# First token block gathered row by row; two dense blocks with some plain fp32 products

## The chip, the cores and the metric

One core of one Trainium2 chip. The metric is the device time of one execution in microseconds. Engines: TensorE (PE) for matrix products, VectorE (DVE) and ScalarE (ACT) for elementwise work, GpSimd (POOL), which here only issues the gathers, and SyncE (SP), which issues the other DMA transfers.

## The reference, cut to what matters

```python
h  = rms_norm(x, norm1_gain)                       # 512 tokens x 1024
A  = dsa_attention(...)                            # sparse attention, indexer picks keys
B  = gated_deltanet(...)                           # chunked, sequential over 64 tokens
x += W_o @ (sigmoid(gA) * (A @ W_A) + sigmoid(gB) * (B @ W_B))
h2 = rms_norm(x, norm2_gain)
# PEER: 8 heads, product keys, top 16 of 128*128 experts per head and token
q  = (h2 @ w_query).reshape(ntok, 8, 2, 128)
s  = einsum('nhpd,hpkd->nhpk', q, sub_keys)        # 128 scores per half
top_s, top_i = top_k(s, 16)                        # per half, then 16 of 16x16 sums
x += sum over the 128 chosen experts e of gate[e] * gelu(h2 . u[e]) * v[e]
```

All of it is fp32. The tables u and v have 16384 rows of 1024 numbers each (64 MB apiece).

## The kernel before, in words

The 512 tokens are four blocks of 128. The program is written with helpers that record each operation; the framework's scheduler then fixes an order for each engine. In place of one plain fp32 product, `mm3` (L91) makes three f32r products from operands that `split` (L167 on ACT, L168 on DVE) cuts into a high and a low part: high x high, high x low, low x high.

- **Projections and chains (first stage).** `fill` is a stream of filler steps: 43 slices of w_in by `mm3`, convolutions, then `attention_branch` (the attention half of the merge, f32r on all 512 tokens). It is interleaved with the four chains (`deltanet` for two pairs of heads, `indexer`, `attender`), FILL_A filler steps for each chain step until the attention's inputs are there, FILL_B after that. `szT` and `qT` hold the chains' results.
- **Merge.** For each of 8 slices the DeltaNet half is multiplied (L709), added (L710), split; then w_o, `second_norm` (L714) for each block, and `hT` (transposed, high and low).
- **Routing.** w_q's products, scores, top 16 of 128 by DVE (L857 to L861), and `choose` (16 best sums, their gates and expert numbers) for each block.
- **Two ways of applying experts.** Blocks 0, 1, 2 are WHOLE: `spread` makes dense gates with one-hot outer products (oa, ob, L983, L986, product `wo`) and writes them to DRAM (gd); `dense_u(i)` multiplies 128 experts' u by the three blocks (24 f32r products of 384 columns) and takes gelu; `dense_v(i)` multiplies the gated activations by 128 rows of v (18 f32r products of 512 columns into six accumulators `acc`). Block 3 is GATHERED: `gathered(s)` fetches, for choice s of each of 128 tokens, one row of 8 KB (u and v side by side) by an indirect DMA of POOL (L951), then a dot (L960) and an addition (L963) on DVE.
- **Order.** AHEAD + KEPT = 62 of the 128 `dense_u` run early (during routing and spread); KEPT = 42 of these write their activations to DRAM (gs) to be read back. The other 66 run in the last stage, spread between the 128 `dense_v`, and so do the gathered rows; U_COST and V_COST space them. Row buffers: ROWS = 4.

Names in the rows: wt, wh, wl a weight tile and its parts; ut, uh, ul those of u; vt, vh, vl those of v; gt, ch, cl the gates; hTh, hTl the input; ya, yh, yl the merge's inputs; row a gathered row; a__ the result of a `dense_u`.

## Time and profile before

| what | value |
|---|---|
| median of 3 runs | 1850.85 us (1849.44 to 1852.79) |
| profiled execution | 1844.26 us, its span 1842.5 us |
| granted clock, mean | 0.998 |
| PE busy | 1791.8 us (97%) |
| DVE busy | 1442.0 us (78%) |
| ACT busy | 803.1 us (44%) |
| DMA moved | 396.74 MB, 215 GB/s on average |

Times are microseconds from the start of the span. "Busy" is the union of an engine's instructions. An instruction's length in the groups contains its latency, so lengths of neighbours overlap. A chain piece "x36" is a run of 36 instructions of one engine. The DMA share is that of 16 DMA engines; it can read slightly over 1.

### The profile page before, as it was taken

The numbers are of one execution on the slowest core, as the hardware profiler recorded it, in microseconds if no ns is written. First come the engines' busy times: TensorE is split into PE (matmuls) and PEld (weight loads), VectorE is DVE, ScalarE is ACT, GpSimd is POOL, SyncE is SP. The second block draws the span as 40 slices with busy tenths as digits, with TensorE's granted clock in tenths as the row PEclk, the third lists the DMA queues.
The fourth block names the chain that finished last, engine by engine and source line by source line (L and its number), as shares of the span: only waits on it lengthen the run. The fifth ranks groups of instructions, "written<-read, shape, count | busy, mean of one in ns | idle before, by whom it ended". The sixth has DMA issues, their size and how long they took to land.

```text
span 1842.5 us, 26292 instructions
## 1 busy us (share of the span) xinstructions
PE 1791.8 (97%) x9527; PEld 1572.5 (85%) x9527; DVE 1442.0 (78%) x3291; ACT 803.1 (44%) x1401; POOL 188.6 (10%) x132
## 2 busy tenths in 40 slices
PE   5999999999999999999999999999999999999998
PEld 4787677878788899999999988888888888888887
DVE  5767988654667899999997686788787887787886
ACT  5433434443533334555655444344443444343442
POOL 0000000000000000010000112122121222212220
PEclk9999999999999999999999999999999999999999
DMA  4211111111643214567676898989988988898974
GB/s 148 92 64 63 58 41 58 52 52 41 211 147 130 89 52 142 186 226 258 250 268 228 307 365 305 336 316 361 337 313 327 347 315 309 335 357 313 343 299 170
DMA packets 142354, 396.74 MB, mean 215 GB/s; under 512 B 10704, under 2 KB 71760, under 8 KB 122768
## 3 DMA queue, kind: packets, MB, share of 16 engines
q1 hardware_dynamic: 123792, 260.84, 40.3%
q0 software_dynamic: 18432, 134.23, 18.9%
q8 instruction: 75, 1.23, 0.3%
q14 instruction: 55, 0.45, 0.1%
HBM read 353.60 MB, written 41.29 MB: 214 GB/s over the span
## 4 chain that ended last, share of the span: by engine, by line
PE 82%; DVE 8%; DMA 6%; ACT 2%; issue 1%; SPq 0%; DVEq 0%; ACTq 0%
PE mm L91 28%; PE acc L91 25%; PE wo L91 6%; PE dn L91 5%; PE at L91 3%; DMA vt<-in_uv_dram 2%; DMA gt<-gd 2%; DVE ul L168 1%; DVE ob L986 1%; PE tr L91 1%; PE at L571 0%; PE dn L320 0%; DMA wt<-in_w_br_dram 0%; DVE tmp L229 0%; DVE gt L1046 0%
## 5 line engine op out<-in xcount | busy, mean ns | idle before, releaser
L91 PE MATMUL acc<-vl,ch 128*128 128x512 f32 x768 | 299.5, 390 | 1.1 <-DVE vl L1045 1.1
L91 PE MATMUL acc<-vh,cl 128*128 128x512 f32 x768 | 298.2, 389 | 0.0
L91 PE MATMUL acc<-vh,ch 128*128 128x512 f32 x768 | 263.1, 390 | 4.9 <-ACT vh L1044 4.9
L951 POOL DMA_INDIRECT row<-in_uv_dram,eidx x124 | 178.6, 1441 | 832.3 <-DVE x1g L963 775.1
L167 ACT CAST uh<-ut 128x1024 fp32r<-128x1024 f32 x128 | 134.6, 1051 | 150.0 <-PE mm L91 84.0
L1045 DVE TENSOR_TENSOR vl<-vt,vh 128x1024 fp32r<-128x1024 f32 x128 | 156.4, 1222 | 50.3 <-ACT vh L1044 47.6
L168 DVE TENSOR_TENSOR ul<-ut,uh 128x1024 fp32r<-128x1024 f32 x128 | 155.9, 1219 | 34.4 <-ACT uh L167 33.8
L91 PE MATMUL mm<-hTh,uh 128*128 128x384 f32 x496 | 168.6, 340 | 2.9 <-ACT gs L818 1.9
L91 PEld LDWEIGHTS acc<-vh,ch 128*128 128x128 f32 x768 | 143.3, 188 | 32.1 <-ACT vh L1044 6.6
L91 PE MATMUL mm<-hTh,ul 128*128 128x384 f32 x496 | 168.0, 340 | 2.7 <-DVE ul L168 2.7
L91 PEld LDWEIGHTS acc<-vl,ch 128*128 128x128 f32 x768 | 144.2, 188 | 30.2 <-DVE vl L1045 2.1
L963 DVE SCALAR_TENSOR_TENSOR x1g<-row,co,x1g 128x1024 f32<-128x1024 f32 x128 | 163.8, 1280 | 7.4 <-ACT co L962 5.3
L91 PEld LDWEIGHTS acc<-vh,cl 128*128 128x128 f32 x768 | 144.1, 188 | 29.2
L1044 ACT CAST vh<-vt 128x1024 fp32r<-128x1024 f32 x128 | 133.9, 1046 | 78.4 <-DMA vt<-in_uv_dram 64.0
L91 PE MATMUL mm<-hTl,uh 128*128 128x384 f32 x496 | 167.3, 337 | 0.0
L167 ACT CAST ch<-gt 128x384 fp32r<-128x384 f32 x128 | 65.5, 512 | 218.1 <-PE acc L91 211.1
L960 DVE CUSTOM_DVE_ANT_0 scr<-row,h2g 128x1024 f32<-128x1024 f32 x128 | 156.0, 1218 | 0.3
L91 PE MATMUL mm<-hh,wh 128*128 128x512 f32 x344 | 144.6, 424 | 3.6 <-ACT hh L167 2.1
L168 DVE TENSOR_TENSOR wl<-wt,wh 128x1024 fp32r<-128x1024 f32 (+1 forms) x81 | 90.1, 1115 | 63.4 <-ACT wh L167 63.2
L91 PE MATMUL mm<-hh,wl 128*128 128x512 f32 x344 | 137.3, 401 | 0.0
L91 PE MATMUL mm<-hl,wh 128*128 128x512 f32 x344 | 136.9, 398 | 0.0
L167 ACT CAST wh<-wt 128x1024 fp32r<-128x1024 f32 (+1 forms) x81 | 77.7, 962 | 110.9 <-PE mm L91 86.7
(818 smaller groups left out, 3765.8 us busy)
## 6 DMA issues: line engine op xcount, KB each, us to landing
ut<-in_uT_dram SPq DMA_DIRECT2D x128, 512.0 KB
vt<-in_uv_dram SPq DMA_DIRECT2D x128, 512.0 KB
gd<-gb SPq DMA_DIRECT2D x24, 1024.0 KB
gt<-gd SPq DMA_DIRECT2D x16, 1536.0 KB
wt<-in_w_in_dram SPq DMA_DIRECT2D x43, 512.0 KB
gs<-gs SPq DMA_DIRECT2D x84, 192.0 KB
wt<-in_w_q_dram SPq DMA_DIRECT2D x16, 512.0 KB
sgd<-tmp SPq DMA_DIRECT2D x16, 256.0 KB
```

Of the source, the lines that this page charges most:

```text
L91: hop[0] = PE.matmul(o, l, r, start=start, stop=stop).ins
L167: S.copy(hi, src)
L168: return V.tensor_tensor(lo, src, hi.bitcast(F32), op=ALU.subtract).ins
L951: G.indirect_dma_start(out=row.rearrange("p t d -> p (t d)"), out_offset=None, in_=uv, in_offset=bass.IndirectOffsetOnAxis(ap=released.get ...
L960: V.tensor_tensor_reduce(scr, row[:, 0], h2g, 1.0, 0.0, op0=ALU.mult, op1=ALU.add, accum_out=a)
L963: V.scalar_tensor_tensor(x1g, row[:, 1], co, x1g, op0=ALU.mult, op1=ALU.add)
L986: V.tensor_scalar(ob[:, t], io, sl[:, 1, n:n + 1], sl[:, 2, n:n + 1], op0=ALU.is_equal, op1=ALU.mult)
L1044: S.copy(vh, vt)
L1045: paced = V.tensor_tensor(vl, vt, vh.bitcast(F32), op=ALU.subtract)
```

## The change

Block 0 leaves the dense blocks: FIRST = 0, WHOLE = (1, 2), GATHERED = 3. `first_block` merges, norms and routes block 0 alone, in the filler stream behind the projections, as soon as the chains have done its tokens, all of it by plain fp32 products (`mm`, one product instead of three); it reads w_br, w_o and w_q a second time (4.2 + 4.2 + 8.4 MB). `first_rows` then gathers block 0's experts: 128 half rows of u (4 KB for each of 128 tokens, 0.5 MB a gather) with a dot on DVE, gelu and gate, 128 half rows of v with an addition. `rows(n)` takes n steps of that stream: it is called in the filler, the merge, the routing, the spread, with each gathered row of block 3, and for what is left at the end. The half rows share four buffers (tag "row").

The dense parts are 256 columns wide now. `dense_u` is 8 plain fp32 products (no split of u); `dense_v` is 12 f32r products, and for every third row (PLAIN = 3, 42 of 128) 4 plain ones without any split. AHEAD 34, KEPT 14. The merge has one loop with both halves on 384 columns, and `attention_branch` is gone.

```diff
-WHOLE, GATHERED = (0, 1, 2), 3
+FIRST, WHOLE, GATHERED = 0, (1, 2), 3
+REST = (*WHOLE, GATHERED)
 NU = len(WHOLE) * P
-FILL_A = 0.85
-FILL_B = 0.6
+NR = len(REST) * P
+FILL_A = 1.0
+FILL_B = 1.3
...
-AHEAD = 20
-KEPT = 42
+AHEAD = 34
+KEPT = 14
...
-V_COST, U_COST = 18 * T, 24 * NU
+V_COST, U_COST = 12 * 227, 16 * 222
+PLAIN = 3
+STEPS = 4
...
+    def first_block():
+        while not done >= {("y", 0, i) for i in range(3)}:
+            yield
+        c = slice(0, P)
+        quarter = lambda n: hp.tile([P, 8, P], F32, name=n, tag="hh", bufs=4)
+        m0 = quarter("m0")
         for dt in range(8):
             s_ = tmp()
-            load(s_, sgd[dt])
-            S.activation(s_, s_, AF.Sigmoid)
-            wt = pp.tile([P, 8, P], F32, name="wt", bufs=2)[:, :4]
-            load(wt, w_br[dt][:, :4])
-            w = [pp.tile([P, 8, P], F32R, name=n, bufs=2)[:, :4] for n in ("wh", "wl")]
-            split(*w, wt)
+            for i in range(2):
+                load(hs(s_, i), sgd[8 * i + dt][:, c])
+            S.activation(s_[:, :2 * P], s_[:, :2 * P], AF.Sigmoid)
+            w = plain(w_br[dt])
...
+                yield
+            V.tensor_tensor(s_[:, :2 * P], s_[:, :2 * P], o[:, :2 * P], op=ALU.mult)
+            V.tensor_tensor(m0[:, dt, :], hs(s_, 0), hs(s_, 1), op=ALU.add)
...
+        for cg in range(2):
+            o = bank("mm")
+            for kp_ in range(4):
+                w = plain(w_o[cg, kp_], (2, T))
+                for k in range(2):
+                    kk = 2 * kp_ + k
+                    mm(o, m0[:, kk, :], w[:, k, :], kk == 0, kk == 7)
+                    yield
+            half = slice(cg * T, (cg + 1) * T)
+            V.tensor_tensor(x1[:, half], x1[:, half], o, op=ALU.add)
...
+        srs = lists[:, 2]
+        for h in range(8):
+            o = bank("mm")
+            for p in range(2):
+                w = plain(w_q[2 * h + p])
+                for k in range(8):
+                    mm(hs(o, p), w[:, k, :], h0[:, k, :], k == 0, k == 7)
+                    if k % 4 == 3:
+                        yield
+            q_ = tmp()
+            load(q_[:, 2 * P:].rearrange("p (l k) -> p l k", k=P), subT[:, 2 * h:2 * h + 2, :])
+            S.copy(q_[:, :2 * P], o[:, :2 * P])
...
+            for p in range(2):
+                t_, i_ = ts[FIRST][:, p, h], ti[FIRST][:, p, h]
+                best(hs(sc, p), t_[:, 0:8], t_[:, 8:16], i_[:, 0:8], i_[:, 8:16], srs[:, p])
...
+        choose(FIRST, new)
...
+        V.scalar_tensor_tensor(first["eu"], flat(sel[FIRST][0]), 256.0, ef, op0=ALU.mult, op1=ALU.add)
...
+    def row_of(s, which):
+        r = ep.tile([P, D], F32, name="row_f", tag="row", bufs=ROWS)
+        G.indirect_dma_start(
+            out=r,
+            out_offset=None,
+            in_=uv2,
+            in_offset=bass.IndirectOffsetOnAxis(ap=first[which][:, s:s + 1], axis=0),
+        )
+        return r
+    def first_rows():
+        a = first["a"]
+        for s in range(P):
+            r = row_of(s, "eu")
+            V.tensor_tensor_reduce(r, r, first["h2"], 1.0, 0.0, op0=ALU.mult, op1=ALU.add, accum_out=a[:, s:s + 1])
+            yield
...
+        for s in range(P):
+            r = row_of(s, "ev")
+            V.scalar_tensor_tensor(first["x1"], r, a[:, s:s + 1], first["x1"], op0=ALU.mult, op1=ALU.add)
+            yield
+        nc.sync.dma_start(out[0:P, :], first["x1"])
...
+    def rows(n):
+        for _ in range(n):
+            next(rows_f, None)
...
         yield from projections()
-        while "mixed" not in done:
-            yield
-        yield from attention_branch()
+        yield from first_block()
+        for _ in range(P):
+            rows(1)
+            for _ in range(STEPS):
+                yield
...
+    while "x1" not in first:
+        next(filler)
...
+        s_ = [tmp() for _ in range(2)]
+        o = [bank("mm")[:, :NR], bank("tr")[:, :NR]]
+        w = weights(pp, w_br[dt])
+        for i in range(2):
+            load(s_[i][:, :NR], sgd[8 * i + dt][:, rest])
+            S.activation(s_[i][:, :NR], s_[i][:, :NR], AF.Sigmoid)
+            for k in range(4):
+                y = (ya[k][:, 0], ya[k][:, 1]) if i == 0 else at(yd, k)
+                mm3(o[i], at(w, 4 * i + k), y, k == 0, k == 3)
+            V.tensor_tensor(s_[i][:, :NR], s_[i][:, :NR], o[i], op=ALU.mult)
+        m_ = s_[0][:, :NR]
+        V.tensor_tensor(m_, m_, s_[1][:, :NR], op=ALU.add)
+        split(mt[0][:, dt, :], mt[1][:, dt, :], m_)
+        rows(2)
...
+        rows(2)
...
+                rows(1)
...
-        ut = up.tile([P, 8, P], F32, name="ut", bufs=2)
+        ut = up.tile([P, 8, P], F32, name="ut", bufs=3)
         load(ut, uT[i])
-        uh = up.tile([P, 8, P], F32R, name="uh", bufs=2)
-        ul = up.tile([P, 8, P], F32R, name="ul", bufs=2)
-        split(uh, ul, ut)
         for k in range(8):
-            mm3(a_, (uh[:, k, :], ul[:, k, :]), (hT[0][:, k, :NU], hT[1][:, k, :NU]), k == 0, k == 7)
+            mm(a_, ut[:, k, :], hT1[:, k, :], k == 0, k == 7)
...
+            rows(1)
...
-        scr = rowq.tile([P, D], F32, name="scr", bufs=1)
-        V.tensor_tensor_reduce(scr, row[:, 0], h2g, 1.0, 0.0, op0=ALU.mult, op1=ALU.add, accum_out=a)
+        V.tensor_tensor_reduce(row[:, 0], row[:, 0], h2g, 1.0, 0.0, op0=ALU.mult, op1=ALU.add, accum_out=a)
...
+            rows(3)
...
     def dense_v(i):
         if i % IC == 0:
-            gt[0] = ex.tile([P, NCH, IC, TC], F32, name="gt", bufs=2)
+            gt[0] = lp.tile([P, NCH, IC, TC], F32, name="gt", tag="big", bufs=2)
             load(gt[0].rearrange("p c i n -> p c (i n)"), gd.rearrange("c p k -> p c k")[:, :, i * TC:(i + IC) * TC])
         g = gt[0][:, :, i % IC, :]
-        vt = ex.tile([P, D], F32, name="vt", bufs=2)
+        vt = ex.tile([P, D], F32, name="vt", bufs=3)
         load(vt, uv[i * P:(i + 1) * P, D:])
+        ge = activations(i)
+        if i % PLAIN == PLAIN - 1:
+            paced = V.tensor_tensor(ge.rearrange("p (c n) -> p c n", n=TC), ge.rearrange("p (c n) -> p c n", n=TC), g, op=ALU.mult)
+            for j, b in enumerate(WHOLE):
+                for c in range(2):
+                    mm(acc[b][c], hs(ge, j), vt[:, c * T:(c + 1) * T], i == 0, i == P - 1)
+            return paced
+        paced = V.tensor_tensor(g, ge.rearrange("p (c n) -> p c n", n=TC), g, op=ALU.mult)
         vh = ex.tile([P, D], F32R, name="vh", bufs=2)
         vl = ex.tile([P, D], F32R, name="vl", bufs=2)
-        S.copy(vh, vt)
-        paced = V.tensor_tensor(vl, vt, vh.bitcast(F32), op=ALU.subtract)
-        V.tensor_tensor(g, activations(i).rearrange("p (c n) -> p c n", n=TC), g, op=ALU.mult)
+        split(vh, vl, vt)
         ch = ex.tile([P, NCH, TC], F32R, name="ch", bufs=2)
         cl = ex.tile([P, NCH, TC], F32R, name="cl", bufs=2)
         split(ch, cl, g)
         chf, clf = (a.rearrange("p c n -> p (c n)") for a in (ch, cl))
-        for b in WHOLE:
+        for j, b in enumerate(WHOLE):
             for c in range(2):
-                mm3(acc[b][c], (hs(chf, b), hs(clf, b)), (vh[:, c * T:(c + 1) * T], vl[:, c * T:(c + 1) * T]), i == 0, i == P - 1)
+                half = slice(c * T, (c + 1) * T)
+                mm3(acc[b][c], (hs(chf, j), hs(clf, j)), (vh[:, half], vl[:, half]), i == 0, i == P - 1)
         return paced
...
+                rows(1)
+    for _ in rows_f:
+        pass
```

How the rows move, engine by engine (before, then now).

**DVE, the end of the last DeltaNet chain.** L329/L330 and L342/L343 start the norm of the last output, rs_t, rs_a, r are the steps of its inverse root, `ot` the output; L849 is the new dot with a gathered half row. Before:

```order
L329 TENSOR_REDUCE s_4139<-s_4137 128x2
L330 TENSOR_SCALAR s_4139<-s_4139 128x2
L159 TENSOR_SCALAR rs_t<-s_4139 128x2
L634 TENSOR_TENSOR mixed<-tmp,mm 128x512
L160 TENSOR_SCALAR r_4142<-rs_t 128x2
L168 TENSOR_TENSOR wl<-wt,wh 128x512
L162 TENSOR_TENSOR rs_a<-r_4142 128x2
L163 SCALAR_TENSOR_TENSOR rs_t<-rs_a,s_4139 128x2
```

Now:

```order
L463 SCALAR_TENSOR_TENSOR szT<-dn_4736,colv,szT 128x2x128
L849 ISA row_f,a_f<-row_f,xe 128x1024
L849 ISA a_f 128x1
L342 TENSOR_REDUCE s_4839<-s_4837 128x2
L849 ISA row_f,a_f<-row_f,xe 128x1024
L849 ISA a_f 128x1
L343 TENSOR_SCALAR s_4839<-s_4839 128x2
L849 ISA row_f,a_f<-row_f,xe 128x1024
L849 ISA a_f 128x1
L171 TENSOR_SCALAR rs_t<-s_4839 128x2
L172 TENSOR_SCALAR r_4842<-rs_t 128x2
```

The dots, each with a read of its sum (L849 ISA a_f), stand between the norm's steps; the first stands one row ahead of these. Of the 128 dots 118 stand ahead of the spread: 10 up to the last step of this chain, the others between the merge's and the routing's rows.

**POOL, the gathers.** Before, 4 and 124 gathers of 8 KB rows and nothing else. Now:

```order
L836 DMA row_f<-in_uv_dram,eu 128x1024 x122
L1117 DMA row<-in_uv_dram,free 128x2048 x4
L1117 DMA row<-in_uv_dram,eidx 128x2048 x6
L836 DMA row_f<-in_uv_dram,eu 128x1024 x4
L1117 DMA row<-in_uv_dram,eidx 128x2048
L836 DMA row_f<-in_uv_dram,eu 128x1024 x2
L1117 DMA row<-in_uv_dram,eidx 128x2048
L836 DMA row_f<-in_uv_dram,ev 128x1024 x2
```

`row_f` is a half row of block 0 (eu from u, ev from v), `row` a whole row of block 3. All 128 half rows of v stand behind the first gathers of block 3; from there on the two kinds alternate until the end.

**PE, the last stage.** `acc` are the accumulators of `dense_v`, `a__` the result of a `dense_u`. Before, a row of u is 24 rows, a row of v 18, of which six stand together:

```order
L91 MATMUL a__11837<-hTh,uh 128x384
L91 MATMUL a__11837<-hTl,uh 128x384
L91 MATMUL a__11837<-hTh,ul 128x384
L91 MATMUL acc_9964<-vh,ch 128x512
L91 MATMUL acc_9965<-vh,ch 128x512
L91 MATMUL acc_9966<-vh,ch 128x512
L91 MATMUL acc_9967<-vh,ch 128x512
```

Now, with two rows of u, a plain row of v and the start of a split one:

```order
L98 MATMUL a__10246<-hT_4878,ut 128x256 x8
L98 MATMUL a__10327<-hT_4878,ut 128x256 x8
L98 MATMUL acc_8694<-vt,ge 128x512
L98 MATMUL acc_8695<-vt,ge 128x512
L98 MATMUL acc_8696<-vt,ge 128x512
L98 MATMUL acc_8697<-vt,ge 128x512
L98 MATMUL acc_8694<-vh,ch 128x512
L98 MATMUL acc_8695<-vh,ch 128x512
```

A row of u takes its operand `ut` straight from the load; a plain row of v takes `vt` and `ge` so.

## Rows read from the trace of the kernel before

**Rows 1.** Windows by stage: us; PE, PEld, DVE, ACT, POOL busy; clock; DMA share; GB/s.
```profile
0.00:487.00 487.00, 460.10 (x2477) 363.89 (x2478) 330.20 (x901) 210.59 (x408) 0.20 (x4) 1.00 0.22 74
487.00:580.00 93.00, 88.87 (x431) 74.96 (x429) 61.01 (x121) 35.86 (x54) 0.00 (x0) 0.98 0.45 158
580.00:755.00 175.00, 171.63 (x923) 157.60 (x922) 159.23 (x832) 67.80 (x108) 0.00 (x0) 0.99 0.31 104
755.00:1030.00 275.00, 270.88 (x1827) 269.58 (x1826) 246.53 (x619) 159.70 (x203) 17.65 (x10) 1.00 0.67 242
1030.00:1842.50 812.50, 800.36 (x3877) 706.42 (x3876) 645.07 (x821) 329.15 (x630) 170.77 (x118) 1.00 0.88 322
```

**Rows 2.** The chain that ended last, by engine.
```profile
PE 82%; DVE 8%; DMA 6%; ACT 2%; issue 1%; SPq 0%; DVEq 0%; ACTq 0%
```

**Rows 3.** The chain in the last stage: start us, us, what.
```profile
1074.99 17.22 DMA vt<-in_uv_dram
```

**Rows 4.** Windows with full DMA engines, and a long one (columns as above).
```profile
1084.00:1094.00 10.00, 9.37 (x48) 8.23 (x47) 5.84 (x12) 1.77 (x3) 0.94 (x1) 1.00 1.01 413
1240.00:1260.00 20.00, 20.00 (x101) 17.99 (x100) 18.57 (x26) 8.89 (x17) 4.52 (x4) 1.00 1.01 401
1030.00:1090.00 60.00, 59.05 (x290) 52.37 (x290) 50.06 (x68) 25.23 (x47) 14.10 (x9) 1.00 1.02 377
1420.00:1620.00 200.00, 199.44 (x974) 177.05 (x973) 159.29 (x202) 81.01 (x156) 48.08 (x32) 1.00 0.89 328
```

**Rows 5.** DMA issues in 1030 to 1090 us: KB each.
```profile
gt<-gd SPq DMA_DIRECT2D x2, 1536.0 KB
```

**Rows 6.** The chain, two pieces of the last stage.
```profile
1441.42 8.16 PE acc L91 x36
1449.58 4.19 PE a__13633 L91 x24
```

**Rows 7.** PE by line and form, first stage: xcount, busy us, mean ns.
```profile
L91 PE MATMUL at<-kT,qT 64*128 64x512 f32 x16 | 9.0, 641 | 0.0
L91 PE MATMUL at<-kT,qT 64*128 64x256 f32 x16 | 5.6, 428 | 0.0
```

**Rows 8.** PE by line and form, 0 to 487 us.
```profile
L91 PE MATMUL mm<-ya,wh 128*128 128x512 f32 x53 | 17.6, 405 | 0.6 <-ACT ya L167 0.3 <-ACT wh L167 0.2
L91 PE MATMUL mm<-ya,wl 128*128 128x512 f32 x26 | 10.2, 398 | 0.0
```

**Rows 9.** DVE by line and form, 580 to 755 us.
```profile
L168 DVE TENSOR_TENSOR ul<-ut,uh 128x1024 fp32r<-128x1024 f32 x18 | 21.8, 1214 | 0.0
L858 DVE FIND_INDEX8 ti<-ts,sc 128x8 uint32<-128x128 f32 x64 | 17.9, 286 | 0.0
L861 DVE MATCH_VALUE_LOAD ti<-ts,sr 128x8 f32 x64 | 4.8, 75 | 0.0
```

**Rows 10.** DVE's timeline at the end of the chains: start us, us, instruction.
```profile
478.02 0.17 DVE L330 TENSOR_SCALAR s<-s 128x2 f32<-128x2 f32 x1
486.16 0.48 DVE L450 SCALAR_TENSOR_TENSOR szT<-dn,colv,szT 128x256 f32<-128x256 f32 x1
```

**Rows 11.** DMA of the last stage, and the landing time of gathered rows.
```profile
DMA packets 98874, 259.93 MB, mean 325 GB/s; under 512 B 5984, under 2 KB 58629, under 8 KB 83717
row<-in_uv_dram,eidx POOLq DMA_INDIRECT x118, 8.7
```

**Rows 12.** DVE by line and form, last stage.
```profile
L1045 DVE TENSOR_TENSOR vl<-vt,vh 128x1024 fp32r<-128x1024 f32 x128 | 156.4, 1222 | 50.3 <-ACT vh L1044 47.6 <-issue 2.3
L963 DVE SCALAR_TENSOR_TENSOR x1g<-row,co,x1g 128x1024 f32<-128x1024 f32 x122 | 156.1, 1280 | 5.2 <-ACT co L962 3.2
L960 DVE CUSTOM_DVE_ANT_0 scr<-row,h2g 128x1024 f32<-128x1024 f32 x122 | 148.6, 1218 | 0.3
L168 DVE TENSOR_TENSOR cl<-gt,ch 128x384 fp32r<-128x384 f32 x128 | 70.9, 554 | 42.9 <-ACT ch L167 42.5
L960 DVE DVE_READ_ACCUMULATOR2_ANT a<- 128x1 f32 x122 | 10.0, 82 | 0.0
```

**Rows 13.** POOL's gathers.
```profile
L951 POOL DMA_INDIRECT row<-in_uv_dram,eidx x124 | 178.6, 1441 | 832.3 <-DVE x1g L963 775.1 <-DVE ob L986 51.6 <-issue 2.7
```

More of the change, by code (lines that the diff above doesn't have):

```diff
@@ new lines, in tile_block, with plain @@
+    x1d = [dr.tile([P, D], F32, name=f"x1d{b}") for b in WHOLE]
+    first = {}
+    uv2 = uv.rearrange("e (t d) -> (e t) d", t=2)
+    turn_w = [0]
+    def plain(src, shape=(8, P)):
+        turn_w[0] += 1
+        n = ("wt", "wh", "wl")[turn_w[0] % 3]
+        w = pp.tile([P, *shape], F32, name=f"p{n}", tag=n, bufs=2)
+        load(w, src)
+        return w
+    def first_block():
[4 more added lines that the diff above has]
+        m0 = quarter("m0")
@@ L630, in attention_branch @@
+        r2 = tiny.tile([P, 1], F32, name="r2e")
+        S.activation(h2, x1, AF.Square, accum_out=s1)
+        V.tensor_scalar(s1, s1, 1.0 / D, EPS, op0=ALU.mult, op1=ALU.add)
+        rsqrt(r2, s1, "e")
+        V.scalar_tensor_tensor(h2, x1, r2, n2g, op0=ALU.mult, op1=ALU.mult)
+        h0 = quarter("h0")
+        for half in range(2):
+            p_ = bank("mm")
             for k in range(4):
-                mm3(o, at(w, k), (ya[:, 0, k], ya[:, 1, k]), k == 0, k == 3)
-                if k < 3:
-                    yield
@@ new lines, in first_block @@
+        sel[FIRST] = [new(f"sel{i}", [P, 8, 16]) for i in range(2)]
+        gate[FIRST] = ep.tile([P, 8, 16], F32, name="gate_f")
+        choose(FIRST, new)
+        ef = new("ef", [P, P])
+        for i, n in enumerate(("eu", "ev")):
+            first[n] = ep.tile([P, P], I32, name=n)
+        V.tensor_scalar(ef, flat(sel[FIRST][1]), 2.0, None, op0=ALU.mult)
+        V.scalar_tensor_tensor(first["eu"], flat(sel[FIRST][0]), 256.0, ef, op0=ALU.mult, op1=ALU.add)
+        V.tensor_scalar(ef, ef, 1.0, None, op0=ALU.add)
@@ L672, in tile_block @@
                     next(filler, None)
-    for _ in filler:
-        pass
+    while "x1" not in first:
+        next(filler)
     show("yaT", qT)
@@ L768, in tile_block @@
                 w[kp_] = weights(pp, w_o[cg, kp_], shape=(2, T))
-            for b in range(NB):
-                with behind(turned[b - NLAG] if b >= NLAG else None):
+            for b in REST:
+                with behind(turned.get(b - NLAG)):
                     for kp_ in range(4):
```

354 lines of the change are left out of this document (202 added, 152 removed).

## The prediction, made before the changed kernel ran

> **What bounds the kernel now.** I read the stages first, from the table of windows [rows 1]. TensorE (PE) is busy 460 of 487 us in the first stage, 89 of 93 in the merge, 172 of 175 in the routing, 271 of 275 while the gates are spread and 800 of 812 in the last stage; the chain of waits says the same, 82% of it on PE [rows 2]. So before, TensorE is the end of every stage. But two other columns of the same table matter for this change: VectorE (DVE) is busy 645 of the last 812 us, and the DMA engines have a share of 0.88 there at 322 GB/s. The chain shows that this share is no longer free cover: at 1075 us PE waits 17.2 us for a row of v [rows 3].
>
> **How fast the DMA engines can go** is read where their share is 1.0 or more [rows 4]: 413 GB/s over 10 us, 401 over 20 us, 377 over 60 us. In the 60 us two of the gate transfers were issued (gt, 1.5 MB, by the code in pieces of 512 bytes) [rows 5]; in the two faster windows none. Over 200 us in which PE was busy 199.4, the rate was 328 GB/s at a share of 0.89.
>
> **Prices on PE.** An f32r product of 512 columns takes 8.16/36 = 0.227 us, one of 384 columns 4.19/24 = 0.174 us [rows 6]. A plain fp32 product shows as two instructions. Their lengths are 641 and 428 ns for 512 and 256 columns [rows 7]; the difference gives 0.213 us of engine time for 256 columns, so 0.427 for 512 and 0.107 for 128. Lengths overlap, so differences and back-to-back pieces are the price, not the lengths.
>
> **The change, part by part.**
>
> *First stage.* Block 0 gets its own merge, w_o, w_q and scores in plain fp32: 64 products of 128 columns for w_br (128 x 0.107 = 14 us), 16 of 512 for w_o (32 x 0.427 = 14), 128 for w_q (256 x 0.107 = 27), 16 for the scores (3): 58 us of PE. Taken away are the attention half's products, which move into the merge: 53 + 26 of 512 columns [rows 8], 79 x 0.227 = 18. Net +40; PE was idle 27 us in this stage, and I let none of it be filled: 527. The bounds are 507 (20 of the 27 idle us get filled) and 555. Block 0's top-16 is a quarter of the 98 us of eight groups, of which the first and the last stand in [rows 9] (17.9 and 4.8), 25 us of DVE, and with its choose about 45, beside 330 of 487 busy: hidden.
>
> The order shows something that the words of the change don't: the first dot with a gathered row stands at the very end of the chains, and 10 dots stand one to one between the tiny steps of the last chain's norm. In the trace those steps lie between 478.0 and 486.2 us [rows 10]. DVE is in order, so each now waits for a gather. One gather's cost from both sides: 8.7 us to land [rows 11] plus a dot of 1.3 over four buffers is 2.5 us; below it is the dot alone, 1.3. I take 2.0 (these rows are 0.5 MB where those were 1 MB): 10 x 2 = 20 us, half of it covered by the merge's first products. +10, with 0 and 25 as ends. The first stage ends at 537.
>
> *Merge and routing* (268 us before). DVE was busy 61 + 159 = 220 [rows 1]. Less 22 for 18 splits of u and 25 for block 0's top-16 [rows 9], plus 10 for the attention half that came in, plus the other 108 of the 118 dots x 1.3 (1.218 and a read of 0.082 [rows 12]) = 140: 323. PE has only some 190 there, since three blocks are left and the first product no longer fills it. DVE is the bound: 355 with 10% for its waits on gathers and on PE (before, it waited 32 of 93 us in the merge and 16 of 175 in the routing); 323 and 400 are the ends. So PE loses its place as the bound here, and the early gathers pay for that.
>
> *Spread* (275 us before). Two blocks in place of three: 256 outer products of 128 columns, 512 x 0.107 = 55, and 31 of the 48 early rows of u: PE 161, DVE about 137. 170 us. Each early row costs 8 fp32 products of 256 columns, 16 x 0.213 = 3.4 us, against 4.19. The last stage starts at 537 + 355 + 170 = 1062 (before 1030).
>
> *Last stage.* PE: 86 rows of v at 12 x 0.227 = 2.72, 42 plain at 8 x 0.427 = 3.41, 80 late rows of u at 3.42 (before 66 at 4.19): 234 + 143 + 274 = 651. DVE: 86 splits of v, 128 products and 86 splits of gates at two thirds of 0.554, 122 gathered rows (1.218 + 0.082 + 1.280), 128 half rows at 1.28 and 10 dots [rows 12]: 680 in lengths, and as lengths overlap (the groups of that view add up to 693, and DVE was busy 645), about 640. Both fall far under 812. DMA does not: 128 rows of v (67.1 MB), 80 of u (41.9), gates 16.8, reloads 1.8, 122 gathered rows of 1 MB (128) and 138 half rows (72.4), **328 MB** against 260 before [rows 11]. At 0.400 that is 820; I take 3.5% more, since the engines' share is below 1 wherever a buffer comes free late: 850 (rate 386). Gate and reload bytes fall from 12% to 6% of the bytes, which is why I sit nearer 401 than 377. The ends are 794 (at 413) and 1000 (at 328). Less 15 for transfers already in flight when the stage starts, plus 10 for a tail in which PE works off the last rows without transfers.
>
> A rule speaks against this change here. In the trace, 60 us ran at 377 GB/s [rows 4]. The Trainium skill, DMA: Bandwidth & Descriptors (Specifications), gives one core some 358 GB/s from HBM; by that the stage would take 916 us in place of 850. The 377 over 60 us do not agree with it.
>
> *Sum.* 1062 + 850 - 15 + 10 = 1907 of span; the profiled execution of before took 1844.26 at a span of 1842.5, so 1909; the median of the shown runs lies 6.6 above the profiled one, so **1915 us** against 1850.85.
>
> *Edits that I cost at nothing:* the third buffers for u and v and the larger AHEAD (34, KEPT 14) only move the start of loads; the final writes of block 0 lie under the last rows of v; POOL's 260 gathers at 1.44 us [rows 13] are 375 us on an engine that does nothing else. If the gathers were throttled by POOL, the price is that of rival 2.
>
> **The rivals.**
>
> 1. *The front hides what it gains* (faster). The early dots go into DVE's waits and the chains' end doesn't feel them: first stage 507, merge and routing 323, spread 161, a start at 991 instead of 1062; the last stage at 0.400 without slack, 820. 991 + 820 - 5 = 1806 of span, 1814 as a median. At that rate it decides from a start before 1027 us; at 850 it would need 997. For: DVE waited 32 of its 93 us in the merge and PE 27 in the first stage. Against: in the routing DVE was already busy 159 of 175, and DVE is in order, so a late gather holds up what is behind it. Chance 0.22, of which 0.04 lands within 0.2% of no change (about what a measurement of this kernel can tell from nothing).
> 2. *The transfers keep the rate that before sustained,* 328 GB/s, as in-order DVE frees row buffers late: 328/0.328 = 1000, so 1062 + 1000 - 5 = 2057 of span, 2065. For: share 0.89 although waits on v were on the chain. Against: there PE, fully busy, set the pace of the loads. Chance 0.07.
> 3. *The first stage's tail gets longer:* the order puts fp32 products of block 0 where f32r filler covered the chains' latency, and routing must end before the chains' last norm. At 65 more: 1980. Chance 0.08.
> 4. *TensorE's clock falls in the last stage.* PE would idle a quarter of it; the stages show a granted clock of 0.98 to 1.00 [rows 1], with PE nearly always busy, so a lower level is not seen. At a mean of 0.75 the 651 become 868, above the 850: only a mean under 0.77 costs anything. With half the stage at 0.5 PE would need 976: 126 more, 2041. Chance 0.04.
> 5. *The short windows at 401 and 413 were bursts,* and what holds over a stage is the 377 of the 60 us: 328/0.377 = 870, with the same 3.5% 901, so 1966. For: no longer stretch was faster. Against: that stretch held the gates. Chance 0.09. (The skill's ceiling, named above, is the stronger form of this: 916 and 1981.)
> 6. *The change does not do what it says:* "early" is not early. The order puts all v half rows and ten of the u ones in the last stage, so 138 of 256 gathers are not early at all. That is in my sum already.
>
> **How the numbers follow.** Forecast (1860 to 1955) 0.50; rival 1 0.22; rivals 2 to 5 0.28. Faster is 0.18 from rival 1; same 0.05 (0.04 of rival 1 and the lower edge of the forecast); slower 0.77. The range leaves out about half of rival 1 below 1835, and rivals 2 and 4 above 2000: some 0.2 in all.
>
> **What would show it.** Right: in the table of stages the last one has a DMA share near 1.0 and 380 to 400 GB/s, PE busy 620 to 680 of some 845, with waits on vt, ut or row on the chain; DVE nearly full between 540 and 900; the last stage's start near 1060. Wrong: a last stage under 790 us or a start before 1000 us (rival 1), a share below 0.9 with idle PE (rival 2), a granted clock below 0.8 (rival 4), or a first stage that ends after 570 (rival 3).

## The result and the profile after

The changed kernel takes 1943.51 us (median of 4 runs, 1935.9 to 1945.83), the kernel before 1850.14 us beside it: a ratio of 1.050, interval 1.046 to 1.054. It is slower by 5%, where 1915 (1835 to 2000) and "slower" were forecast. The profiled execution's span is 1940.1 us, 97.6 more than before's 1842.5.

The table of windows of the changed kernel, cut where the first dot with a gathered row, the spread and the second product begin (columns as in [rows 1]):

```profile
0.00:541.00 541.00, 510.44 (x2852) 409.71 (x2852) 368.34 (x1140) 221.06 (x429) 3.71 (x8) 0.98 0.30 100
541.00:900.00 359.00, 257.55 (x1217) 231.22 (x1218) 320.44 (x1063) 84.14 (x142) 146.11 (x119) 0.82 0.76 267
900.00:1048.00 148.00, 148.00 (x933) 137.08 (x932) 117.01 (x307) 72.89 (x104) 17.44 (x10) 1.00 0.80 283
1048.00:1940.10 892.10, 724.36 (x2678) 531.46 (x2676) 635.68 (x822) 203.74 (x500) 370.39 (x252) 0.90 0.96 366
```

The cut at 541 us, the first dot, is not the mark that ends the first stage in [rows 1]: there the last chain has done its last step (szT at 486.16 [rows 10]). The same step stands at 563.83 us now, ten dots after the first one, and PE is busy only 2 of the 23 us between the two marks:

```profile
563.83 0.47 DVE L463 SCALAR_TENSOR_TENSOR szT<-dn,colv,szT 128x256 f32<-128x256 f32 x1
```
```profile
541.00:564.30 23.30, 2.09 (x8) 2.12 (x9) 14.69 (x36) 1.35 (x3) 11.47 (x11) 0.54 0.82 287
564.30:900.00 335.70, 255.46 (x1211) 229.11 (x1210) 305.75 (x1028) 82.79 (x139) 134.64 (x109) 0.84 0.76 265
```

So against [rows 1], by the same mark: first stage +77 (564 against 487), merge and routing +68 (336 against 93 + 175), spread -127 (148 against 275), last stage +80 (892 against 812): +98 in all. The gain that two dense blocks in place of three bring stands in the spread; the other three stages give back more. PE is busy 510 of the 541 us before the first dot and all of the spread; from 541 to 900 DVE is busy 320 of 359 us; in the last stage the DMA engines are busy 0.96 of the time. In the runs below, "merge and routing" starts at the first dot, as in the table, so it contains the chain's end. The chain that ended last has PE with 44%, where [rows 2] had 82%:

```profile
PE 44%; DVE 20%; DMA 19%; issue 11%; POOL 3%; ACT 3%; SPq 0%; DVEq 0%; POOLq 0%; ACTq 0%
```

The last stage in two parts, and what the DMA queues moved in it (compare [rows 11]: 260 MB at 325 GB/s):

```profile
1048.00:1660.00 612.00, 532.45 (x2094) 408.64 (x2093) 423.57 (x559) 141.45 (x363) 248.95 (x171) 0.93 0.99 380
1660.00:1940.10 280.10, 191.90 (x585) 122.82 (x583) 212.11 (x264) 62.29 (x139) 121.44 (x81) 0.84 0.88 333
```
```profile
DMA packets 102780, 326.09 MB, mean 366 GB/s; under 512 B 8007, under 2 KB 42845, under 8 KB 87508
```

For 612 us the engines are full at 380 GB/s; behind that their share falls to 0.88, though 93 MB are still to come, so what they lack there is a request. The waits in the last stage name a suspect. First two waits of the changed kernel, then the one of the kernel before (who, what for, us in total, times, the longest):

```profile
DVE gt L1215 <- DMA gt<-gd: 66.1, 8, 13.2
...
DVE ge L1210 <- DMA gt<-gd: 38.7, 4, 10.9
```
```profile
DVE gt L1046 <- DMA gt<-gd: 43.9, 10, 8.7
```

DVE waits 105 us for gates, before 44; 74 of the 105 fall in the 612 us in which the engines were full all the same, 30 in the 280 us behind. Loads of gates are 23% of the chain of the last stage. On the chain it looks like this, the two longest pieces of 1048 to 1240 us:

```profile
1107.90 31.19 DMA gt<-gd
...
1167.68 27.72 DMA gt<-gd
```

A load of gates brings eight rows into one of two buffers. It is issued when the load before the previous one has been split for the last time, and DVE's first multiplication with it stands 28 to 31 us behind the issue in the two pieces shown, 13 to 31 us in the fourteen loads from 1107 us on. DVE works in a fixed order: behind its wait stand the dots and additions that free the row buffers, and with them the next gathers.

The end of the last chain, on DVE's timeline (before: [rows 10]):

```profile
540.95 1.23 DVE L849 CUSTOM_DVE_ANT_0 row_f<-row_f,xe 128x1024 f32<-128x1024 f32 x1 [1.81 <-DMA row_f<-in_uv_dram,eu]
...
542.10 0.48 DVE L463 SCALAR_TENSOR_TENSOR szT<-dn,colv,szT 128x256 f32<-128x256 f32 x1
546.35 1.23 DVE L849 CUSTOM_DVE_ANT_0 row_f<-row_f,xe 128x1024 f32<-128x1024 f32 x1 [3.76 <-DMA row_f<-in_uv_dram,eu]
```

So the chain's steps do stand behind gathered rows, as the order said, up to the last one at 563.83 us.

### The profile page after: what moved, and what is told of

Its sections match the earlier page's. It is cut to its first block, busy times and chain, and to the rows that moved or that the text cites. A ratio compares the mean times of both kernels' runs of the same rounds, so it can differ in the third digit from the quotient of the medians.

```text
span 1940.1 us, 22532 instructions
## 1 busy us (share of the span) xinstructions
PE 1640.3 (85%) x7676; PEld 1309.5 (67%) x7676; DVE 1441.5 (74%) x3330; ACT 581.8 (30%) x1173; POOL 537.7 (28%) x388
## 4 chain that ended last, share of the span: by engine, by line
PE 44%; DVE 20%; DMA 19%; issue 11%; POOL 3%; ACT 3%; SPq 0%; DVEq 0%; POOLq 0%; ACTq 0%
PE mm L98 21%; DMA gt<-gd 11%; PE acc L98 6%; DMA row_f<-in_uv_dram,eu 4%; PE dn L98 4%; PE at L98 3%; PE wo L98 3%; DVE x1g L1128 2%; POOL row_f L836 2%; DVE row_f L849 2%; DVE row L1125 2%; DVE xe L856 2%; DVE vl L180 1%; DMA vt<-in_uv_dram 1%; DVE wl L180 1%
## 5 line engine op out<-in xcount | busy, mean ns | idle before, releaser
L836 POOL DMA_INDIRECT row_f<-in_uv_dram,eu x128 | 156.8, 1225 | 735.6 <-DVE attT L426 536.1
L836 POOL DMA_INDIRECT row_f<-in_uv_dram,ev x128 | 168.4, 1316 | 286.2 <-DVE xe L856 264.3
L98 PE MATMUL acc<-vt,ge 128*128 128x512 f32 x336 | 162.1, 628 | 41.4 <-DMA vt<-in_uv_dram 41.4
L98 PE MATMUL mm<-hT,ut 128*128 128x256 f32 x768 | 177.2, 385 | 3.8 <-ACT ge L1060 3.3
L849 DVE CUSTOM_DVE_ANT_0 row_f<-row_f,xe 128x1024 f32<-128x1024 f32 x128 | 155.4, 1218 | 31.1 <-DMA row_f<-in_uv_dram,eu 30.6
L98 PE MATMUL acc<-vl,ch 128*128 128x512 f32 x344 | 148.6, 432 | 22.6 <-DVE vl L180 22.3
L856 DVE SCALAR_TENSOR_TENSOR xe<-row_f,a_f,xe 128x1024 f32<-128x1024 f32 x128 | 163.8, 1280 | 4.8 <-DMA row_f<-in_uv_dram,ev 4.5
L1125 DVE CUSTOM_DVE_ANT_0 row<-row,h2g 128x1024 f32<-128x1024 f32 x128 | 156.3, 1221 | 4.1 <-DMA row<-in_uv_dram,eidx 4.1
L98 PE MATMUL acc<-vh,ch 128*128 128x512 f32 x344 | 114.6, 447 | 52.2 <-ACT vh L179 51.1
L98 PE MATMUL acc<-vh,cl 128*128 128x512 f32 x344 | 142.4, 417 | 0.0
```

Source lines behind the costliest of these rows:

```text
L98: hop[0] = PE.matmul(o, l, r, start=start, stop=stop).ins
L836: G.indirect_dma_start(out=r, out_offset=None, in_=uv2, in_offset=bass.IndirectOffsetOnAxis(ap=first[which][:, s:s + 1], axis=0),)
L849: V.tensor_tensor_reduce(r, r, first["h2"], 1.0, 0.0, op0=ALU.mult, op1=ALU.add, accum_out=a[:, s:s + 1])
L856: V.scalar_tensor_tensor(first["x1"], r, a[:, s:s + 1], first["x1"], op0=ALU.mult, op1=ALU.add)
L1125: V.tensor_tensor_reduce(row[:, 0], row[:, 0], h2g, 1.0, 0.0, op0=ALU.mult, op1=ALU.add, accum_out=a)
```

## The experiments

The theory at the start, **A**: the last stage is bound by the bytes that the DMA engines carry. Against it, **B**: it is bound by DVE's waits, for gates above all, which in its fixed order hold up all that stands behind them; and **C**: by PE at a lower granted clock. The framework's scheduler fixes the order from its own estimate, so most edits also move rows; in the runs 4 and 5 the order on every engine is that of their parent. Runs 1 to 3 leave out a part of the work to see what it costs.

**1. Half of v's bytes.**

```diff
-        vt = ex.tile([P, D], F32, name="vt", bufs=3)
-        load(vt, uv[i * P:(i + 1) * P, D:])
+        vt = ex.tile([P, T], F32, name="vt", bufs=3)
+        load(vt, uv[i * P:(i + 1) * P, D:D + T])
...
-        split(vh, vl, vt)
+        split(two(vh), two(vl), vt[:, None].to_broadcast([P, 2, T]))
```

Expected: 

> The changed kernel, but each of the 128 rows of v is loaded with 512 of its 1024 columns (0.25 MB in place of 0.5 MB) and used twice; every instruction of PE, DVE and ACT keeps its size. This leaves out half of v, so the result is not the reference's. Theory A (the last stage is bound by the bytes that the DMA engines carry, 320 MB at 366 GB/s in 880 us): 33.5 MB less at 366 to 385 GB/s, 87 to 92 us off, about 1850. Theory B (the last stage is bound by DVE's in-order waits for gates and gathered rows, which have landing times and not bytes as their cause): under 30 us off, 1910 or more. Theory C (TensorE at its lower granted clock, 713 us of busy PE plus its waits): no more than 40 us off, since PE's work is unchanged.

Measured in one run: 1887.9 us, 56 off. The last stage:

```profile
1042.50:1886.10 843.60, 710.68 (x2683) 526.91 (x2681) 634.06 (x822) 201.82 (x501) 361.71 (x252) 0.92 0.93 347
```

48 of the 56 us are in this stage: more than B or C allow, about half of what A asks. The rate fell with the bytes (366 to 347 GB/s, share 0.96 to 0.93), and DVE still waited 87 us for gates. Bytes matter, but something else holds the engines up as well.

**2. Without block 0's gathers.**

```diff
-        r = ep.tile([P, D], F32, name="row_f", tag="row", bufs=ROWS)
-        G.indirect_dma_start(...)
-        return r
+        if "still" not in first:
+            first["still"] = [ep.tile([P, D], F32, name="row_f", tag="row", bufs=ROWS) for _ in range(ROWS)]
+            for r in first["still"]:
+                V.memset(r, 0.0)
+        return first["still"][s % ROWS]
```

Expected: 

> The changed kernel without block 0's 256 gathers: the dots and additions of DVE stay and read four buffers that are set to zero once, so the experts of block 0 are left out of the result. In the last stage some 70 MB less are moved. Theory A: 70/0.385 = 180 us off the last stage, down to about 700, where PE (650 to 710) is the next bound. Theory B: if landing times of block 0's rows are what DVE waits for, much the same; if it is the gates' landing, 50 us off at most. For the front: if DVE's own work binds merge and routing (320 of 359 us busy), they take 325 to 345 us without the gathers; if the waits on gathers bind them, they fall under 300. In all about 1740 by A.

Measured in one run: 1836.77 us, 107 off. The windows of merge and routing, and of the last stage:

```profile
541.00:902.00 361.00, 293.31 (x1541) 264.15 (x1540) 293.95 (x1165) 109.55 (x195) 0.00 (x0) 0.83 0.31 98
...
1062.50:1834.90 772.40, 693.61 (x2683) 517.42 (x2681) 631.13 (x822) 203.30 (x501) 198.72 (x118) 0.95 0.90 332
```

120 us came off the last stage for 70 MB, where A said 180: with 256 MB left, PE (694 of 772 busy) is next to the bound. On the front the run says nothing: without gathers to wait for block 0's lists, the scheduler put that block's routing later (its list of rows was written at 649 us in place of 535), so the window holds other work.

**3. Dots of 8 columns.**

```diff
-            V.tensor_tensor_reduce(r, r, first["h2"], 1.0, 0.0, ...
+            V.tensor_tensor_reduce(r[:, :8], r[:, :8], first["h2"][:, :8], 1.0, 0.0, ...
```

Expected: 

> The changed kernel with all 256 gathers, but the 128 dots of block 0 read 8 of the 1024 columns (0.1 in place of 1.2 us each), so block 0's u product is left out. Theory: DVE's work on the early dots is what lengthens merge and routing (359 us against 268 before); then they fall by 100 to 130 us, to 230 to 260, unless the gathers' own pace (4 buffers) holds the dots up, then they stay over 300. The last stage is not shorter than 860 by theory A, as its bytes are the same or more. In all about 1830 to 1850.

Measured in one run: 1860.37 us, 83 off, where 1830 to 1850 was expected. Merge and routing, the spread, and the last stage:

```profile
541.00:797.00 256.00, 217.47 (x1140) 197.04 (x1140) 189.02 (x1017) 80.58 (x140) 114.10 (x110) 0.95 0.92 338
797.00:970.00 173.00, 169.84 (x1023) 155.36 (x1022) 129.25 (x363) 76.09 (x111) 26.29 (x22) 0.99 0.81 299
970.00:1858.60 888.60, 721.46 (x2683) 526.57 (x2681) 625.28 (x822) 203.61 (x501) 355.85 (x252) 0.91 0.96 367
```

Merge and routing fell by 103 us, from 359 to 256, for 131 us less of DVE's work, although nearly as many gathers passed (338 GB/s there). So the early dots cost most of what their DVE time says, and the early gathers as such cost little. The spread took 25 of the 103 back (148 to 173), as more products stood in it. The last stage stayed at 889, the same bytes at the same rate.

**4. Gates read in one piece.** Only the layout of `gd` in DRAM changes: the small pieces (512 bytes) stand on the write's side, in the spread.

```diff
-    gd = dr.tile([NCH, P, P * TC], F32, name="gd")
+    gd = dr.tile([P // IC, P, NCH, IC * TC], F32, name="gd")
...
-            nc.sync.dma_start(gd[WHOLE.index(b) * (P // TC) + c], gb.rearrange("p i n -> p (i n)"))
+            nc.sync.dma_start(gd[:, :, WHOLE.index(b) * (P // TC) + c, :].rearrange("g p k -> p g k"), gb.rearrange("p (g i) n -> p g (i n)", i=IC))
...
-            load(gt[0].rearrange("p c i n -> p c (i n)"), gd.rearrange("c p k -> p c k")[:, :, i * TC:(i + IC) * TC])
+            load(gt[0].rearrange("p c i n -> p (c i n)"), gd[i // IC].rearrange("p c k -> p (c k)"))
```

Expected: 

> The changed kernel with another layout of the gates in DRAM: written in pieces of 512 bytes, read back as 8 KB in one piece for each partition (before: written in 8 KB, read in pieces of 512 bytes). Instructions of all engines and their order are the same. DVE waited 105 us for the gates in the last stage, and they are 24% of its chain. Theory B (these waits set the end): 50 us off or more, 1890 or less. Theory A (bytes set the end): the 16.8 MB in small pieces cost at 290 instead of 400 GB/s some 16 us, so 5 to 20 us off, about 1930.

Measured: 1883.56 us, ratio to before 1.020 (1.017 to 1.023) where the change had 1.050. So 60 us came off, what B expected. The windows of spread and last stage, and the one wait for gates that is left:

```profile
900.00:1050.00 150.00, 150.00 (x945) 138.85 (x944) 119.42 (x314) 72.05 (x103) 17.44 (x10) 1.00 0.90 282
1050.00:1876.90 826.90, 714.82 (x2681) 524.92 (x2679) 636.39 (x822) 204.69 (x501) 368.31 (x252) 0.94 0.99 395
```
```profile
DVE gt L1215 <- DMA gt<-gd: 15.1, 3, 11.7
```

The same 326 MB now pass in 827 us at a share of 0.99 and 395 GB/s. From the shares, the engines worked 0.96 x 892 = 856 us on them in the changed kernel, and 0.99 x 827 = 819 now: of the 65 us some 37 were work of the DMA engines and some 28 time in which they stood idle (the shares are rounded to 0.01, so each is good to about 8 us). Not all of the 37 are in the small pieces: the gathered rows have a queue of their own (packets, MB, share; first the changed kernel, then this run), and their same 194 MB took 0.549 x 892 = 490 us beside the small pieces and 0.578 x 827 = 478 without them.

```profile
q0 software_dynamic: 36288, 194.00, 54.9%
...
q0 software_dynamic: 36288, 194.00, 57.8%
```

That the idle 28 come from DVE's waits is read from POOL's, whose gathers wait for the additions (xe) to free a buffer: 65 us less in this run (again first the changed kernel).

```profile
POOL row_f L836 <- DVE xe L856: 264.3, 63, 23.1
...
POOL row_f L836 <- DVE xe L856: 199.1, 63, 21.2
```

On the write's side the share of the spread rose from 0.80 to 0.90, about 15 us of the engines, at no cost, since PE is full there. Neither A nor B alone was right: the small pieces made the bytes dearer, and DVE's wait for them held up other requests. The edit changes the length of the pieces and their spacing in DRAM (512 bytes out of every 8 KB) together; which of the two made them dear stays open.

**5. The same layout in the kernel before.**

Expected: 

> The kernel before with the gates' layout of the run before this one (written in pieces of 512 bytes, read in 12 KB). DVE waited 44 us for the gates in its last stage, the chain of waits names them with 2% (37 us). PE was busy 800 of 812 us there, so no more than some 12 us can come off; if the waits had slack 0 to 4 us, 1848. If the small writes disturb the spread (DMA share 0.67, the writes of 24 MB become small), up to 10 us slower.

Measured: 1840.14 us, ratio 0.9989 (0.9976 to 1.0002): no difference that can be told from none. DVE's wait for gates fell from 44 to 15 us there too:

```profile
DVE gt L1046 <- DMA gt<-gd: 15.4, 6, 3.8
```

PE was busy 800 of 812 us in that stage, so the wait had slack, as the expectation allowed. The layout stood in the kernel before, and became a cost only when the DMA engines became the bound.

**6. The front in plain fp32.** On top of run 4, merge, w_o and w_q of blocks 1 to 3 lose their splits:

```diff
-                mm3(o[i], at(w, 4 * i + k), y, k == 0, k == 3)
+                mm(o[i], w[:, 4 * i + k, :], y[:, k, rest], k == 0, k == 3)
...
-            mm3(o[:, c], at(w, k), tuple(t[:, k, c] for t in hT), k == 0, k == 7)
+            mm(o[:, c], w[:, k, :], hT1[:, k, c], k == 0, k == 7)
...
-                mm3(acc[b], at(mt, kk, col(b)), at(w[kp_], k), kk == 0, kk == 7)
+                mm(acc[b], mt[:, kk, col(b)], w[kp_][:, k, :], kk == 0, kk == 7)
```

Expected: 

> The changed kernel with the gates' layout of the fourth run (read in one piece) and, besides, the merge, w_o and w_q products of blocks 1 to 3 in plain fp32, so without their splits: some 52 us less for DVE in merge and routing (38 splits at 1.22 us and smaller ones), 31 us more for PE, which had room there (254 of 359 us busy). Theory: DVE binds merge and routing, so these fall from 359 to 305 to 320 us and the whole from 1884 to about 1835; the last stage stays at 820 to 835, bound by bytes. Rival: the pace of the gathers (4 buffers, 118 gathers in 359 us) or PE at its lower granted clock (0.83 there) binds them; then they stay over 340 and the whole at 1870 or more.

Measured: 1845.18 us, 0.9998 (0.9978 to 1.0019) of before. Merge and routing, the spread, and the last stage:

```profile
541.00:872.00 331.00, 279.19 (x1035) 189.38 (x1033) 277.16 (x1003) 51.51 (x106) 130.83 (x118) 0.92 0.81 286
872.00:1012.00 140.00, 138.91 (x888) 128.76 (x887) 121.49 (x323) 71.42 (x101) 18.53 (x10) 1.00 0.90 287
1012.00:1840.00 828.00, 715.87 (x2679) 523.56 (x2677) 636.47 (x822) 203.60 (x500) 362.55 (x252) 0.94 0.99 394
```

359 became 331, not 305 to 320: DVE works 41 us less than in run 4 (318), but is now only 277 of 331 us busy. Another 10 us came off the spread (150 to 140). The three longest transfers on the chain of merge and routing, and the wait that they belong to, show the next bound:

```profile
582.87 8.87 DMA row_f<-in_uv_dram,eu
664.14 9.39 DMA row_f<-in_uv_dram,eu
...
788.90 9.58 DMA row_f<-in_uv_dram,eu
...
DVE row_f L849 <- DMA row_f<-in_uv_dram,eu: 49.0, 51, 2.9
```

**7. More rows of u ahead.** `KEPT = 30`, `HEAD = 16, 4` on top of run 6.

Expected: 

> The run before this one, with 16 more rows of u ahead of the last stage (KEPT 30 in place of 14, 16 of them ahead of the first choose). The last stage moves 16 x (0.52 - 0.13) = 6.3 MB less and computes 16 rows of u less (55 us of PE). Theory (bytes bind the last stage, 395 GB/s): 16 us off that stage. In the front 55 us of PE are added: nothing if they fill PE's idle time in the routing, 55 if they stand in the spread, where PE is full. In all between 15 faster and 40 slower than the run before; about 1830.

Measured: 1884.56 us, 39 more. The added rows of u all went into the spread, where PE is full:

```profile
872.00:1068.00 196.00, 194.63 (x1145) 177.54 (x1144) 123.07 (x323) 76.57 (x117) 12.74 (x10) 1.00 0.83 258
1068.00:1883.50 815.50, 675.12 (x2423) 483.70 (x2421) 637.83 (x822) 197.75 (x484) 367.12 (x252) 0.91 0.98 392
```

The spread grew from 140 to 196, 56 for 16 rows of 3.4; the last stage lost 12, for 6 MB. PE's 41 us less there brought nothing else. So C falls for the stage as run 6 has it, with the gates read in one piece.

**8. All rows of v split** (`PLAIN = 1000` on top of run 4).

Expected: 

> The changed kernel with the gates read in one piece (1884 us) and without plain fp32 rows in the second product: all 128 rows of v are split. DVE has 42 x (1.22 + 0.42) = 69 us more in the last stage (636 becomes 705 of 827), PE 29 us less, the bytes are the same. Theory (bytes): within 10 us of 1884. Rival (DVE, in order, sets the pace of the row buffers): 30 to 70 us more.

Measured in one run: 1909.04 us, 25 more. The last stage:

```profile
1052.00:1907.00 855.00, 703.66 (x2854) 559.41 (x2852) 697.53 (x906) 260.18 (x585) 372.78 (x252) 0.93 0.96 382
```

28 us for 61 us more of DVE's work: between A (10 at most) and its rival (30 or more). The bytes are the same and the engines' share fell from 0.99 to 0.96, so most of the 28 us are idle time of the engines. That fits DVE's order pacing the requests even where the engines are nearly full; with one run, it is not shown beyond that. The plain rows of v are worth something after the change.

**9. The plain rows of v alone, in the kernel before.**

```diff
+        if i % 3 == 2:
+            ge = activations(i)
+            paced = V.tensor_tensor(ge..., ge..., g, op=ALU.mult)
+            for b in WHOLE:
+                for c in range(2):
+                    mm(acc[b][c], hs(ge, b), vt[:, c * T:(c + 1) * T], i == 0, i == P - 1)
+            return paced
```

Expected: 

> The kernel before with one part of the change alone: every third row of the second product in plain fp32 without splits. PE has 42 x (12 x 0.427 - 18 x 0.227) = 44 us more, DVE 42 x (1.22 + 0.55) = 74 us less. As PE bounds the last stage there (800 of 812 us busy): 44 us slower, 1890. If DVE's relief takes PE's waits away: 30 us slower. It would show that this part pays only where PE has room, as after the change.

Measured in one run: 1907.02 us, 62 more than before's 1845.34, where 44 were expected. PE is busy 860 of 883 us in the last stage:

```profile
1022.00:1905.00 883.00, 860.21 (x3692) 674.04 (x3691) 577.38 (x738) 278.42 (x553) 157.30 (x118) 0.99 0.83 299
```

Over the whole program PE is busy 1842 us in place of 1792: 50 of the 62 us are its work, near the price of 44, and the rest is time in which it waits. So a part that helps in one kernel (run 8) costs 3% in the other.

**10. Six row buffers.** On top of run 6, every fifth and sixth half row gets a buffer of a second pool.

```diff
+        if "lp" not in first or s % (ROWS + MOREROWS) < ROWS:
+            r = ep.tile([P, D], F32, name="row_f", tag="row", bufs=ROWS)
+        else:
+            r = first["lp"].tile([P, D], F32, name="row_f", tag="row_f", bufs=MOREROWS)
```

Expected: 

> The run with the front in plain fp32 (1845 us), with six row buffers for block 0's half rows in place of four. There the chain of merge and routing was 26% landing of half rows, 14% dots, 9% gather issues: 118 dots in 331 us, 2.8 us each, about a fourth of landing plus dot plus issue (8 + 1.3 + 1). Theory: this ring is the bound, so six buffers bring the pace to some 1.8 us and merge and routing to DVE's own work (277 us busy): 285 to 305 us, the whole to 1805 to 1820. Rival: PE at its lower clock (279 of 331 us busy) or DVE's order binds them: over 320, the whole above 1835. The last stage stays at 820 to 835 in both, as its bytes are the same.

Measured: 1840.21 us, 0.9968 (0.9951 to 0.9986) of before. Merge and routing fell from 331 to 314, between the theory's 285 to 305 and its rival's 320 and more; the whole stayed above 1835, as the rival said. Merge and routing, the spread, and DVE's wait for gathered rows:

```profile
541.00:855.00 314.00, 265.67 (x989) 179.78 (x988) 272.12 (x1001) 50.37 (x103) 138.86 (x120) 0.92 0.83 300
855.00:1005.00 150.00, 148.16 (x933) 136.78 (x932) 123.75 (x325) 73.55 (x103) 18.57 (x10) 1.00 0.89 280
...
DVE row_f L853 <- DMA row_f<-in_uv_dram,eu: 22.3, 23, 2.3
```

The ring of buffers was a part of the bound: DVE's wait for half rows fell from 49 to 22 us. Of its other 20 idle us the waits name PE for some 15. The spread took 10 of the 17 us back (140 to 150), as its products rose from 888 to 933.

**11. Rows still earlier.** On top of run 10, more steps of block 0's rows in the program:

```diff
-        rows(2)
+        rows(3)
...
-        rows(2)
+        rows(4)
...
-            rows(3)
+            rows(2)
...
-            rows(1)
+            rows(3)
```

Expected: 

> The run before this one, with more steps of block 0's rows called for in the merge and the routing: all 128 half rows of u and 36 of v stand ahead of the spread in DVE's order, where 118 and none stood. The last stage moves 46 x 0.52 = 24 MB less. Theory (bytes at 395 GB/s bind the last stage): 61 us off it, 827 to about 766, while merge and routing get 10 x 1.3 + 36 x 1.28 = 59 us of DVE's work, of which some lies in its waits: 30 to 60 longer. In all 0 to 30 us faster than the run before, 1780 to 1815. Rival (the last stage is bound by DVE's order and PE's waits, too): no more than 30 us off that stage, and the whole no faster than the run before.

Measured: 1835.24 us, 0.9940 (0.9923 to 0.9957) of before. This run and run 10 are the only ones with all of the work whose interval lies below the kernel before. Merge and routing, spread, last stage:

```profile
546.00:920.00 374.00, 314.00 (x1166) 218.58 (x1165) 330.62 (x1068) 54.72 (x115) 193.63 (x166) 0.91 0.91 332
920.00:1042.00 122.00, 117.47 (x784) 109.48 (x783) 119.94 (x318) 69.81 (x94) 18.34 (x10) 1.00 0.96 307
...
1042.00:1832.00 790.00, 702.54 (x2647) 520.69 (x2645) 580.96 (x762) 200.91 (x497) 296.53 (x204) 0.94 0.95 379
```

The last stage lost 39 us (829 to 790) for 26 MB, where bytes alone would give 65: its share is down to 0.95 and PE is busy 703 of 790. Merge and routing grew by 60 and start 5 later, and the spread gave 28 back. So in the profiled executions 37 us stand against 39: work that is moved ahead is paid for there almost in full.

**12. More bytes.** On top of run 4, each row of v brings 0.25 MB that nobody reads.

```diff
+        more = ex.tile([P, T], F32, name="more", bufs=2)
+        load(more, uv[i * P:(i + 1) * P, :T])
```

Expected: 

> The changed kernel with the gates read in one piece (1884 us, last stage 827 us at 395 GB/s), and with each row of v a further 0.25 MB that nothing reads: 33.5 MB more in the last stage, no instruction more on PE, DVE or ACT. Theory (bytes bind the last stage): 33.5/0.395 = 85 us more, about 1968. Rival (the order of waits among DVE, ACT and PE binds it, and the DMA engines are full only because they wait for nothing): 40 us or less, under 1925.

Measured: 1950.99 us (2 runs), 67 more than run 4 (62 more when each is set against the kernel before beside it, 1851.67 and 1846.42); the last stage:

```profile
1052.00:1952.80 900.80, 727.31 (x2683) 519.34 (x2681) 637.40 (x822) 205.91 (x501) 352.17 (x252) 0.93 1.00 400
```

74 us more in the stage at a share of 1.00, with no work added on any other engine; 85 were expected, the rival allowed 40. Some 8 of the missing 11 are the room that a share of 0.99 had left. So with the gates read in one piece, bytes bind the last stage: 360 MB at 400 GB/s are the 901 us.

## Why the prediction was right

Step by step, in spans; the first stage ends with the last step of the last chain, as in [rows 1]:

| step | forecast | measured | forecast is off by |
|---|---|---|---|
| first stage ends | 537 | 564 | -27 |
| merge and routing | 355 | 336 | +19 |
| spread | 170 | 148 | +22 |
| last stage starts | 1062 | 1048 | +14 |
| last stage | 845 | 892 | -47 |
| span | 1907 | 1940 | -33 |

What it had right is the direction and the two new bounds, DVE in merge and routing and DMA in the last stage. That the total came within 2% is partly luck: two stages were forecast too short and two too long. Of its own signs, the DMA share (0.96), DVE's 320 of 359 us and the start at 1048 came; the rate of 380 to 400 GB/s (366), PE's 620 to 680 us (724) and a chain of waits on vt, ut or row (gates, with 23%) did not.

**First stage.** Up to the first dot the forecast had 527 us, and it was 541: PE's work grew by 50 (460 to 510) in place of 40. The order was read rightly, and the price of 20 us for the ten dots was close to the measured 23. What failed is the overlap: half of it was to be covered by the merge's first products, and PE was busy 2 of the 23 us.

**Merge and routing.** DVE took PE's place as the bound, with 306 us of work in 336 (323 in 355 forecast). Run 3 shows that it is the dots; runs 6 and 10 that a ring of four buffers stands close behind, which the forecast had only as a price of one gather and within its 10% of waits.

**Spread.** 22 us too long. The early rows of u were counted there as 31; the stage's 148 us less 55 for the outer products are 27 rows of 3.4. The price itself was right:

```profile
1157.33 3.45 PE a__9499 L98 x16
```

**Last stage.** Bytes (328 forecast, 326 measured), DVE's work (640, 636) and PE's (651 at full clock; 724 measured, and 651/0.90 is 723) were right, and that DMA would bind it too. The term that failed is the rate: "I take 3.5% more" for the queues' empty time gave 386 GB/s, and it was 366. The forecast saw that the gates' small pieces lower the rate (the 60 us at 377), and concluded that with their share of the bytes halved this would fade. Run 4 shows the opposite: with the gates in one piece the stage takes 827 us at 395 GB/s, close to the 820 without any slack. The 65 us of that run are more than the 47 that the forecast lacked; some 37 are work of the DMA engines and some 28 their idle time. The chain of the kernel before names DMA gt<-gd with 2%, and this was not carried into the sum.

One reading of the kernel before was wrong, though no term hangs on it. The forecast says that "at 1075 us PE waits 17.2 us for a row of v" [rows 3]. That piece of the chain is the time of a transfer, and PE was busy through all of it:

```profile
1074.99:1092.21 17.22, 17.22 (x85) 15.17 (x84) 11.57 (x16) 4.30 (x9) 2.81 (x3) 1.00 1.05 402
```

**The rivals.** Rival 1 (the front hides its gains) fell with the chain's end at 564 and the last stage's start at 1048, 21 us behind the later of its two thresholds (997 and 1027). Rival 2's mechanism, buffers that DVE frees late, is in the 47 us, far from its price. Rival 3 missed its sign, an end after 570, by 6 us: the first stage's tail did grow, but 23 us of it are the ten dots, and not the products that this rival names. Rival 4 half came true: the granted clock was 0.82 from 541 to 900 us and 0.90 in the last stage, where PE was busy 258 of 359 and 724 of 892 us, but run 7 took 41 us of PE's work out of the last stage and got 12 us for 6 MB less. In merge and routing no run changed the clock alone, so what the lower clock costs there stays open. Rival 5 (bursts) fell: run 12 held 400 GB/s for 901 us. The Trainium skill (DMA: Bandwidth & Descriptors, Specifications) gives a limit of some 358 GB/s for one core; these 400 GB/s do not agree with it. The Trainium skill (the same page, Measured) has 425 GB/s for a core whose neighbour is idle; no run here reached that over a stage.
